# A hybrid encoder on one core: output-weight splits placed behind the last pair's first scores, and one weight sum made by an adding transfer

## The chip, the core and the metric

The kernel runs on one core of a Trainium2 chip. The metric is the device time of one execution in microseconds (us), the median of several runs. A core has TensorE (PE, matmuls; PEld loads the stationary operand), VectorE (DVE), ScalarE (ACT), GpSimd (POOL) and SyncE (SP), each with its own queue of instructions that it works through in order. Transfers are issued from SP and POOL here and run on the core's DMA engines.

## What is computed

Two layers on x of 512 x 1024 floats; layer 0 has mixer A, layer 1 mixer B, and each mixer is followed by a squared-ReLU MLP:

```python
for i in range(2):
    h = rms_norm(x, norm_mix[i])
    x = x + (dilated_mixer if i == 0 else mla_mixer)(h, ...)
    h = rms_norm(x, norm_ffn[i])
    a = relu(h @ ffn_w1[i])
    x = x + (a * a) @ ffn_w2[i]
```

Mixer A projects h to q, k and v of three head groups (8 heads of 128 in each), attends in dilated windows and merges the groups. Mixer B projects to low-rank latents, makes q, k and v of 8 heads from them, scales q and k by their norms, attends over all 512 positions, and multiplies the heads' outputs with b_w_o (1024 x 1024).

## The kernel before, in words

A float32 product is made of three matmuls of rounded operands: each operand is split into a high part (hi, rounded by a copy on ACT, `whi`) and the rest (lo, a subtraction on DVE, `wlo`), and hi·hi, lo·hi and hi·lo are summed in the same bank of PSUM. Lines 157 and 158 make the splits of most weights (`load_unit`), lines 406 and 407 those of mixer A's v weights (`split_w`), line 185 is the matmul of the general projection, line 421 that of the v products.

**Mixer A's v projection** (`v_phase`). The v of a group's heads 0 to 5 is h (512 x 1024) times a 1024 x 768 weight, and it is done by seven products of half-size blocks instead of eight (Strassen's scheme). The weight blocks are b11, b12, b21, b22, each 128 x 4 x 384 on chip (768 KB), loaded by two SP transfers of 384 KB (line 328). `add_block` (line 334) makes sums of blocks with two additions on DVE. In `piece`, for group 0, `bT` holds b11 + b12 for product 5, then has b22 added for product 6, and last b21 for product 4 (the last two in place); product 7 takes b3 = b12 + b22. Ssp0 to Ssp3 are the split sums on the side of h. `put` (lines 438, 440) evacuates the banks into vo, and POOL transfers vo to memory (line 444). The v of head 6, of all three groups at once, is an ordinary projection, whose `raw` weight tiles come by line 145 and whose results (v6) go out by three POOL transfers (line 501). The tiles of the blocks share a set of six buffers ("wq"): a block is loaded when the last reader of an older block has been issued and is done.

**Mixer B** works by pairs of heads. `score` (lines 1105 to 1121) takes one head and 128 rows: five matmuls (three kn, qn; two kr, qr) into one bank, the row-max on DVE (line 1116), its scaling (1117), the exponential on ACT (1119), which reads the bank, and the normalization on DVE (1120, 1121). `part2` transposes the result on PE and copies it to pTs (1130 on ACT, 1132 on DVE); `pv_b` multiplies it with v (1138) and splits the head's output into oB (1140 on ACT, 1141 on DVE). A loop over all scores runs `part2` three scores behind, and makes the next pair's keys and queries between (`kv_chunk`, with ks on line 1086; `q_chunk`, with qn and qr on 1069 to 1073). For the last pair `bank` gives the scores two banks ("sc"), for the others it takes "acc" banks. Then `project` (line 1191) multiplies oB with b_w_o, in units of 128 x 2 x 512: SP loads raw (line 147), ACT and DVE split it (157, 158), and PE adds up the unit's matmuls (185) in four "acc" banks.

**What sets the order.** The program text is recorded and a scheduler then orders the instructions of each engine; a step that is written later can be put earlier where its data and buffers allow. `tc.issue_after(x)` holds a block of the text back: what it holds may not be put ahead of the instruction x on x's engine. The splits of the first b_w_o units, written last, were put among the instructions of the earlier pairs this way.

Of the kernel before, what the change touches and what calls it, by code (L numbers as in the profile page):

```python
# [12 lines left out]
AF = mybir.ActivationFunctionType  # L13
ALU = mybir.AluOpType
AX = mybir.AxisListType
# [4 lines left out]
NT = S // P  # L20
# [4 lines left out]
HB = 8  # L25
# [62 lines left out]
def encoder_kernel(ctx: ExitStack, tc: tile.TileContext, x, norm_mix, norm_ffn, a_w_qkv, a_q_gain, a_k_gain,  # L88
                   a_w_o, b_w_in, b_q_a_gain, b_w_qb, b_kv_a_gain, b_w_kvb, b_q_gain, b_k_gain, b_w_o,
                   ffn_w1, ffn_w2, consts, out):  # L90
    nc = tc.nc
    V, A, G, PE = nc.vector, nc.scalar, nc.gpsimd, nc.tensor
    uid = [0]
    marks = {}

    def nm(s):
        uid[0] += 1
        return f"{s}_{uid[0]}"
# [24 lines left out]
    def transpose(o, i):  # L123
        PE.transpose(o, i, ident)  # L124
# [182 lines left out]
    def v_phase(vp):  # L307
# [23 lines left out]
        def add_block(t, x, y):  # L331
            for u in range(2):
                us = slice(2 * u, 2 * u + 2)
                V.tensor_tensor(t[:, us], x[:, us], y[:, us], op=ALU.add)
# [5 lines left out]
        b11, b21, bT, b12, b22 = {}, {}, {}, {}, {}  # L340
# [83 lines left out]
        def both(p, w, banks, first):  # L424
            for u, t in ((0, 0), (0, 1), (1, 0), (1, 1)):
                product(p, w, banks, first, u, t)

        def new_banks(chain):
            pl, tg = {"a": (sc_p, "sc"), "b": (tp_p, "tp"), "d": (acc_p, "acc")}[chain]
            return [pl.tile([P, 512], F32, tag=tg, name=nm(tg)) for _ in range(2)]  # L430

        def put(g, i, n, how, banks, last):

            o = vo[:, 2 * i + n]
            for t in range(2):
                acc = banks[t][:, :VH]
                if how == "set":
                    A.activation(o[:, t], acc, AF.Copy)
                else:
                    marks["put"] = V.tensor_tensor(o[:, t], o[:, t], acc,  # L440
                                                   op=ALU.add if how == "add" else ALU.subtract).ins
                if last:

                    nc.gpsimd.dma_start(vall[g].rearrange("(m r) d -> m r d", r=NT)
                                        [:, 2 * i + t, VH * n:VH * n + VH], o[:, t])

        def piece(g, ba):

            bb = new_banks("b")
            both(5, bT[g], bb, True)  # L450
            put(g, 1, 1, "set", bb, False)
            add_block(bT[g], bT[g], b22[g])
            both(3, b22[g], bb, False)
            put(g, 0, 1, "set", bb, False)
            b3 = vp.tile([P, 4, VH], F32, tag="h32", name=nm("b3"))
            add_block(b3, b12[g], b22[g])
            both(6, bT[g], ba, False)
            put(g, 0, 1, "sub", ba, True)
            add_block(bT[g], bT[g], b21[g])
            both(7, b3, ba, False)  # L460
            put(g, 1, 1, "sub", ba, True)
            both(4, bT[g], ba, False)
            put(g, 1, 0, "set", ba, True)
# [47 lines left out]
        for i in range(2):  # L511
            split_s(2, dif[:, 1, i], i)
        piece(0, ba)

        rot = vp.tile([P, D], F32, tag="xn", name="rot", bufs=2)
# [435 lines left out]
    if True:  # L951
        with tc.tile_pool(name="bpool", bufs=1, reuse_waits="tile") as bp, \
# [66 lines left out]
            def bank(d, which):  # L1019

                pool, tag = {"s": (sc_p, "sc"), "p": (tp_p, "tp"), "o": (tp_p, "tp")}[which] \
                    if d["p"] == HB // 2 - 1 else (acc_p, "acc")
                return pool.tile([P, 512], F32, tag=tag, name=nm(tag))
# [82 lines left out]
            def score(d, h, r):  # L1106

                qn, qr, kn, kr = d["qn"][r], d["qr"][r], d["kn"], d["kr"]
                rq = d["rq"][:, r, h:h + 1]
                sc = bank(d, "s")  # L1110
                ops = [(qn[:, h, 0], kn[:, h, 0]), (qn[:, h, 0], kn[:, h, 1]), (qn[:, h, 1], kn[:, h, 0]),
                       (qr[:, h], kr[:, h, 0]), (qr[:, h], kr[:, h, 1])]
                for i, (lt, rt) in enumerate(ops):
                    PE.matmul(sc, lhsT=lt, rhs=rt, start=(i == 0), stop=(i == 4))  # L1114
                mx = st.tile([P, 4], F32, tag="bmx", name=nm("bmx"))
                V.tensor_reduce(mx[:, 0:1], sc, axis=AX.X, op=ALU.max)
                V.tensor_scalar(mx[:, 1:2], mx[:, 0:1], rq, -1.0, op0=ALU.mult, op1=ALU.mult)
                pe = bw.tile([P, S], F32, tag="pe", name=nm("pe"), bufs=3)
                A.activation(pe, sc, AF.Exp, bias=mx[:, 1:2], scale=rq, accum_out=mx[:, 2:3])
                V.reciprocal(mx[:, 3:4], mx[:, 2:3])  # L1120
                V.tensor_scalar(pe, pe, mx[:, 3:4], None, op0=ALU.mult)

                def part2(pT):
                    tp = bank(d, "p")
                    for j in range(NT):
                        transpose(tp[:, j * P:(j + 1) * P], pe[:, j * P:(j + 1) * P])
                    tv = tp.rearrange("p (j t) -> p j t", j=NT)
                    dst = pT[:, :, r * P:(r + 1) * P]
                    if r % 2:
                        A.activation(dst, tv, AF.Copy)  # L1130
                    else:
                        V.tensor_copy(dst, tv)
                return part2
# [27 lines left out]
            for s_ in range(HB * NT + lag):  # L1161
                p, c = divmod(s_, 8)
                if s_ < HB * NT:
                    if c == 0 and p:
                        cur = nxt
                    pend.append((cur, c // 4, c % 4, score(cur, c // 4, c % 4)))
                if s_ >= lag:
                    d, h2, r2, f = pend.pop(0)
                    if r2 == 0:
                        if pTs is None:  # L1170
                            pTs = x16.tile([P, 2, NT, S], F32, tag="x16", name="pTs")
                        pT = pTs[:, h2]
                    f(pT)
                    if r2 == NT - 1:
                        pv_b(d, h2, pT)
                if p + 1 < HB // 2:
                    if c == 2:
                        nxt = new_pair(p + 1)
                    if s_ < NT - 1:
                        tail = tail + [q_chunk(cur, s_ + 1)]  # L1180
                    fresh = [fn(nxt, r) for fn, r in plan.get(c, [])]
                    if c == 7:
                        tail, fresh = tail + fresh, []
                    for f in tail:
                        f()
                    tail = fresh

    bh = ctx.enter_context(tc.tile_pool(name="bh", bufs=1, reuse_waits="tile"))
    hT = bh.tile([P, KD, 2, S], F32R, name="hT_f1")
    with tc.tile_pool(name="po1", bufs=1, reuse_waits="tile") as po:  # L1190
        project(oB, b_w_o[0], resid, norm_ffn[1:2, :].rearrange("o d -> (o d)"), hT, po, "g_ffn1")
    with tc.tile_pool(name="mlp1", bufs=1, reuse_waits="tile") as mp:
        mlp(1, ffn_w1[1], ffn_w2[1], hT, resid, mp, lambda r, c: nc.sync.dma_start(
# [33 lines left out]
```

## Time and profile before

| | us |
|---|---|
| median of 3 runs | 1429.62 |
| lowest, highest | 1429.39, 1430.68 |
| the profiled execution | 1427.53 |
| its span | 1425.8 |
| PE busy | 1394.0 |
| DVE busy | 939.6 |
| ACT busy | 740.5 |
| POOL busy | 217.2 |

The span runs from the first instruction to the last in the profile; the execution's time has 1.73 us more. Times of single instructions are counted from the span's start. Matmuls overlap: of a row of matmuls the distance from start to start tells the cost of one (0.17 us for 384 columns, 0.23 for 512), not its duration. The same holds on DVE and ACT, where an instruction begins some 0.08 us before the one ahead of it has ended. A number in square brackets after an instruction is the time for which its engine was idle before it, with what ended the idle time.

### The profile page before, as it was taken

The page shows a single profiled execution, that of the slowest core. Times are in us where ns is not written, and L with a number is a line of the kernel's source. Part 1 is how long each engine was busy: PE and PEld are TensorE (multiplying, and loading weights), DVE is VectorE, ACT ScalarE, POOL GpSimd, SP SyncE. Part 2 cuts the span into 40 slices and gives each one's busy share as a digit, 9 for nine tenths or more (in the row PEclk, how much of TensorE's full clock was granted, in tenths as well). Part 3 has the DMA queues.
Part 4 walks back from the last instruction along what each step waited for, and adds up shares of the span by engine and source line. Part 5 has one row for each costly group of instructions (what it writes and reads, how often), then busy time and mean ns, then how long its engine had stood idle before and what let it go on. Part 6 is the DMA issues. An engine that isn't in the chain of part 4 may idle for free.

```text
span 1425.8 us, 19234 instructions
## 1 busy us (share of the span) xinstructions
PE 1394.0 (98%) x7044; PEld 1183.8 (83%) x7044; DVE 939.6 (66%) x1497; ACT 740.5 (52%) x1594; POOL 217.2 (15%) x240
## 2 busy tenths in 40 slices
PE   7999999999999999999999999999999999999998
PEld 7999888988888988888888887777768888888886
DVE  6886768676886754465564759788745365575647
ACT  6554656464564623553545446677633553544543
POOL 1110212021112001020010203433201020020201
PEclk9999999999999999999999999999999999999999
DMA  9535222322322335668493844200115658394835
GB/s 323 166 134 168 75 87 87 107 89 75 118 61 77 121 134 195 174 133 222 116 233 99 206 120 91 82 31 30 44 40 163 183 127 231 93 234 128 192 90 118
DMA packets 121086, 185.25 MB, mean 130 GB/s; under 512 B 8416, under 2 KB 58336, under 8 KB 120992
## 3 DMA queue, kind: packets, MB, share of 16 engines
q1 hardware_dynamic: 101808, 144.96, 31.6%
q0 software_dynamic: 19184, 39.07, 15.2%
q8 instruction: 55, 0.90, 0.3%
q14 instruction: 39, 0.32, 0.1%
HBM read 176.13 MB, written 7.86 MB: 129 GB/s over the span
## 4 chain that ended last, share of the span: by engine, by line
PE 89%; DVE 6%; ACT 2%; issue 1%; DMA 1%; POOL 0%; SPq 0%; DVEq 0%; ACTq 0%; POOLq 0%
PE acc L185 51%; PE sc L852 11%; PE tp L852 7%; PE tp L124 4%; PE sc L421 3%; PE acc L1138 1%; PE sc L1032 1%; PE acc L1114 1%; PE tp L421 1%; DVE wlo L796 1%; PE sco L701 1%; PE sc L587 1%; PE acc L421 1%; PE sco L697 1%; DVE wlo L407 1%
## 5 line engine op out<-in xcount | busy, mean ns | idle before, releaser
L185 PE MATMUL acc<-whi,hT 128*128 128x512 f32 (+2 forms) x1216 | 384.2, 390 | 2.2 <-ACT hT L739 1.3
L185 PE MATMUL acc<-hT_f,whi 128*128 128x512 f32 (+1 forms) x1152 | 318.7, 366 | 1.7 <-DVE resid L915 1.2
L158 DVE TENSOR_TENSOR wlo<-raw,whi 128x1024 fp32r<-128x1024 f32 (+3 forms) x146 | 172.4, 1189 | 180.2 <-ACT whi L157 179.9
L185 PEld LDWEIGHTS acc<-whi,hT 128*128 128x128 f32 x1216 | 225.4, 188 | 42.0 <-ACT hT L739 1.9
L185 PEld LDWEIGHTS acc<-hT_f,whi 128*128 128x128 f32 x1152 | 208.1, 189 | 37.4 <-DVE resid L915 1.6
L185 PE MATMUL acc<-wlo,hT 128*128 128x512 f32 (+2 forms) x608 | 235.9, 388 | 0.0
L157 ACT ACTIVATE whi<-raw 128x1024 fp32r<-128x1024 f32 (+3 forms) x146 | 149.7, 1031 | 161.5 <-PE acc L185 64.1
L796 DVE TENSOR_TENSOR wlo<-wqs,whi 128x1024 fp32r<-128x1024 f32 x112 | 137.9, 1232 | 113.4 <-ACT whi L795 113.4
L185 PE MATMUL acc<-hT_f,wlo 128*128 128x512 f32 (+1 forms) x576 | 204.9, 366 | 0.0
L795 ACT ACTIVATE whi<-wqs 128x1024 fp32r<-128x1024 f32 x112 | 118.8, 1061 | 161.3 <-PE acc L185 65.8
L852 PE MATMUL sc<-whi,asp 128*128 128x512 f32 x512 | 164.9, 390 | 0.8 <-DVE resid L826 0.7
L781 POOL DMA_DIRECT2D wqs<-in_ffn_w_dram x64 | 77.6, 1344 | 546.1 <-DVE wlo L796 362.4
L185 PEld LDWEIGHTS acc<-wlo,hT 128*128 128x128 f32 x608 | 114.4, 188 | 18.7 <-issue 0.2
L185 PEld LDWEIGHTS acc<-hT_f,wlo 128*128 128x128 f32 x576 | 108.5, 189 | 17.4
L852 PE MATMUL tp<-whi,asp 128*128 128x512 f32 x352 | 112.2, 390 | 1.8 <-DVE resid L826 1.8
L852 PEld LDWEIGHTS sc<-whi,asp 128*128 128x128 f32 x512 | 96.1, 188 | 21.4 <-issue 1.5
L132 POOL TENSOR_TENSOR qrs<-rs_v,nhalf 128x4 f32<-128x4 f32 x48 | 58.7, 1228 | 288.8 <-DVE rs_v L129 239.7
L852 PE MATMUL sc<-wlo,asp 128*128 128x512 f32 x256 | 99.6, 389 | 0.0
L137 ACT ACTIVATE junk<-acc 128x128 f32<-128x128 f32 x192 | 53.0, 276 | 56.4 <-PE acc L185 51.4
L852 PEld LDWEIGHTS tp<-whi,asp 128*128 128x128 f32 x352 | 66.1, 188 | 16.4 <-DVE resid L826 2.7
L852 PE MATMUL tp<-wlo,asp 128*128 128x512 f32 x176 | 68.2, 389 | 0.0
L295 ACT ACTIVATE qkT<-tp 128x512 f32<-128x512 f32 x48 | 35.8, 765 | 51.2 <-PE tp L124 50.9
(231 smaller groups left out, 2185.3 us busy)
## 6 DMA issues: line engine op xcount, KB each, us to landing
wqs<-in_ffn_w_dram SPq DMA_DIRECT2D x80, 512.0 KB, 5.1
raw<-in_ffn_w_dram SPq DMA_DIRECT2D x64, 512.0 KB, 4.5
wqs<-in_ffn_w_dram POOLq DMA_DIRECT2D x64, 512.0 KB, 7.5
raw<-in_a_w_qkv_dram SPq DMA_DIRECT2D x96, 256.0 KB, 3.1
b<-in_a_w_qkv_dram SPq DMA_DIRECT2D x24, 384.0 KB, 5.7
vall<-vo POOLq DMA_DIRECT2D x24, 192.0 KB, 2.2
raw<-in_a_w_o_dram SPq DMA_DIRECT2D x8, 512.0 KB, 3.8
raw<-in_b_w_o_dram SPq DMA_DIRECT2D x8, 512.0 KB, 3.7
```

Of the source, the lines that this page charges most:

```text
L124: PE.transpose(o, i, ident)
L132: G.tensor_tensor(out, v[:, :n], nhalf[:, :n], op=ALU.pow)
L137: A.activation(junk, x, AF.Square, scale=1.0 / math.sqrt(dim), accum_out=out)
L157: A.activation(hi[:, :nk, :n], raw[:, :nk, :n], AF.Copy)
L158: V.tensor_tensor(lo[:, :nk, :n], raw[:, :nk, :n], hi[:, :nk, :n].bitcast(F32), op=ALU.subtract)
L185: PE.matmul(accs[o][:, oc], lhsT=lt, rhs=rt, start=(kt == 0 and p_i == 0 and hv == 0), stop=(kt == total - 1 and p_i == 2), skip_group_che ...
L295: A.activation(dst, tv, AF.Copy)
L421: PE.matmul(banks[t][:, :VH], lhsT=lt, rhs=rt[:, j], start=(first and k == 0 and i_ == 0), stop=(k == 3 and i_ == 2), skip_group_check=True)
L781: marks["sum"] = nc.gpsimd.dma_start(t, src, accum_op=ALU.add).ins
L795: A.activation(hi, x, AF.Copy)
L796: V.tensor_tensor(lo, x, hi.bitcast(F32), op=ALU.subtract)
L852: PE.matmul(bk[t], lhsT=lt, rhs=rt[:, j], start=(first and k == 0 and i_ == 0), stop=(k == 3 and i_ == 2), skip_group_check=True)
```

## The change

Two edits, in `piece` and around the last `project`:

```diff
             put(g, 0, 1, "sub", ba, True)
-            add_block(bT[g], bT[g], b21[g])
+            if g:
+                add_block(bT[g], bT[g], b21[g])
+            else:
+                for u in range(2):
+                    nc.gpsimd.dma_start(bT[g][:, 2 * u:2 * u + 2], wblk(g, 1, 0, u), accum_op=ALU.add)
             both(7, b3, ba, False)
...
-                V.tensor_reduce(mx[:, 0:1], sc, axis=AX.X, op=ALU.max)
+                marks["max"] = V.tensor_reduce(mx[:, 0:1], sc, axis=AX.X, op=ALU.max).ins
...
-                A.activation(pe, sc, AF.Exp, bias=mx[:, 1:2], scale=rq, accum_out=mx[:, 2:3])
+                marks["exp"] = A.activation(pe, sc, AF.Exp, bias=mx[:, 1:2], scale=rq, accum_out=mx[:, 2:3]).ins
...
                     pend.append((cur, c // 4, c % 4, score(cur, c // 4, c % 4)))
+                    if s_ == HB * NT - 8:
+                        last_pair = marks["max"], marks["exp"]
...
-    with tc.tile_pool(name="po1", bufs=1, reuse_waits="tile") as po:
+    with tc.tile_pool(name="po1", bufs=1, reuse_waits="tile") as po, \
+            tc.issue_after(last_pair[0]), tc.issue_after(last_pair[1]):
         project(oB, b_w_o[0], resid, norm_ffn[1:2, :].rearrange("o d -> (o d)"), hT, po, "g_ffn1")
```

The first edit: in group 0 the last of bT's three sums is made by two transfers that read b21 again from memory and add it into bT, issued on POOL (line 464 of the changed file); each reads and writes a half of bT. b21 is then read last by product 2, its buffer is free earlier, and SP's load of group 1's b11 stands ahead of the last raw of the head-6 projection. The second edit: the row-max (DVE) and the exponential (ACT) of the last pair's first score are remembered, and no instruction of the last `project` on these two engines may stand ahead of them.

DVE in group 0, from the split of bT for product 6 on. `b_70` is b3, `b_4` b21, `bT_671` and `b_110` belong to group 1; sc_154 and sc_155 are the banks of products 6, 7 and 4. Before:

```order
L407 TENSOR_TENSOR wlo_546<-bT_384,whi_545 128x2x384
L387 TENSOR_TENSOR Ssp_116<-dif,Ssp_116 128x4x128
L407 TENSOR_TENSOR wlo_562<-bT_384,whi_561 128x2x384
L334 TENSOR_TENSOR bT_384<-bT_384,b_4_122 128x768 x2
L407 TENSOR_TENSOR wlo_584<-b_70_542,whi_583 128x2x384
L334 TENSOR_TENSOR bT_671<-b_84_662,b_85_665 128x768 x2
L407 TENSOR_TENSOR wlo_600<-b_70_542,whi_599 128x2x384
L440 TENSOR_TENSOR vo<-vo,sc_154 128x384
L407 TENSOR_TENSOR wlo_620<-bT_384,whi_619 128x2x384
L440 TENSOR_TENSOR vo<-vo,sc_155 128x384
L407 TENSOR_TENSOR wlo_636<-bT_384,whi_635 128x2x384
L334 TENSOR_TENSOR b_110_824<-b_85_665,b_86_668 128x768 x2
```

and now:

```order
L407 TENSOR_TENSOR wlo_546<-bT_384,whi_545 128x2x384
L334 TENSOR_TENSOR b_70_542<-b_9_143,b_10_146 128x768 x2
L407 TENSOR_TENSOR wlo_562<-bT_384,whi_561 128x2x384
L387 TENSOR_TENSOR Ssp_116<-dif,Ssp_116 128x4x128
L334 TENSOR_TENSOR bT_671<-b_84_662,b_85_665 128x768 x2
L407 TENSOR_TENSOR wlo_584<-b_70_542,whi_583 128x2x384
L440 TENSOR_TENSOR vo<-vo,sc_154 128x384
L407 TENSOR_TENSOR wlo_600<-b_70_542,whi_599 128x2x384
L407 TENSOR_TENSOR wlo_620<-bT_384,whi_619 128x2x384
L440 TENSOR_TENSOR vo<-vo,sc_155 128x384
L334 TENSOR_TENSOR b_110_824<-b_85_665,b_86_668 128x768 x2
L407 TENSOR_TENSOR wlo_636<-bT_384,whi_635 128x2x384
```

The additions bT<-bT,b_4 are gone; b3's additions stand behind the wlo of bT's first half instead of ahead of it (in the first list they are the step just above); wlo_620 and wlo_636 split bT for product 4, and a vo stands behind each.

ACT at the start of the last pair, where pe is the exponential, qn and qr are copies of the transposed queries, and hT the output of the head before. Before:

```order
L1140 ACTIVATE hT_8026<-acc_9574 128x512
L1047 ACTIVATE qs_9486<-sc_9472 128x256
L1069 ACTIVATE qn_9447<-tp_9442,gn 128x2x128
L1072 ACTIVATE qr_9448<-tp_9442 128x256
L1069 ACTIVATE qn_9500<-tp_9495,gn 128x2x128
L1072 ACTIVATE qr_9501<-tp_9495 128x256
L1119 ACTIVATE pe_9526,bmx_9523<-sc_9517,bmx_9523,rqs_76 128x512
L1069 ACTIVATE qn_9511<-tp_9506,gn 128x2x128
L157 ACTIVATE whi_9853<-raw_9851 128x1024
```

and now:

```order
L1145 ACTIVATE hT_8026<-acc_9574 128x512
L1074 ACTIVATE qn_9500<-tp_9495,gn 128x2x128
L1074 ACTIVATE qn_9511<-tp_9506,gn 128x2x128
L1077 ACTIVATE qr_9501<-tp_9495 128x256
L1077 ACTIVATE qr_9512<-tp_9506 128x256
L1124 ACTIVATE pe_9526,bmx_9523<-sc_9517,bmx_9523,rqs_76 128x512
L157 ACTIVATE whi_9725<-raw_9723 128x1024
L157 ACTIVATE whi_9755<-raw_9753 128x1024
L157 ACTIVATE whi_9785<-raw_9783 128x1024
```

The first exponential stood ahead of the last qn and qr and now stands behind both qr; the first three whi of b_w_o, which stood some 30 instructions and more further up, follow it.

PE at the same place: sc_9517, sc_9536 and sc_9555 are the first three scores, acc_9719 to 9722 the four banks of the last projection. Before, around the first score:

```order
L185 MATMUL acc_9720<-whi_9725,hT_8026 128x512
L185 MATMUL acc_9720<-wlo_9726,hT_8026 128x512
L185 MATMUL acc_9720<-whi_9725,hT_8026 128x512
L1114 MATMUL sc_9517<-kn_9160,qn_9387 128x512 x3
L185 MATMUL acc_9720<-whi_9725,hT_8026 128x512
L185 MATMUL acc_9720<-wlo_9726,hT_8026 128x512
```

and now, around the third:

```order
L1119 MATMUL sc_9536<-kr_9161,qr_9448 128x512 x2
L1119 MATMUL sc_9555<-kn_9160,qn_9500 128x512 x3
L1119 MATMUL sc_9555<-kr_9161,qr_9501 128x512 x2
L124 MATMUL tp_9594<-ck,pe_9526 128x128 x4
L185 MATMUL acc_9719<-whi_9725,hT_8026 128x512
L185 MATMUL acc_9720<-whi_9725,hT_8026 128x512
L185 MATMUL acc_9721<-whi_9725,hT_8026 128x512
```

The L185 matmuls stood among the scores, from right behind p·v (line 1138) on, and now begin behind the third score and the first transposes of an exponential; the first two scores' kn matmuls now stand ahead of the p·v of the pair before.

## Rows read from the trace of the kernel before

**Rows 1.** The page, parts 1, 2 and 4: totals, granted clock by slice, chain.

```profile
PE 1394.0 (98%) x7044; PEld 1183.8 (83%) x7044; DVE 939.6 (66%) x1497; ACT 740.5 (52%) x1594; POOL 217.2 (15%) x240
...
PEclk9999999999999999999999999999999999999999
...
PE 89%; DVE 6%; ACT 2%; issue 1%; DMA 1%; POOL 0%; SPq 0%; DVEq 0%; ACTq 0%; POOLq 0%
```

**Rows 2.** Busy time by stretch: us, PE, PEld, DVE, ACT, POOL, PEclk, DMA share, GB/s.

```profile
40.00:45.00 5.00, 5.00 (x31) 5.00 (x30) 5.00 (x7) 3.97 (x6) 2.06 (x3) 1.00 0.17 49
...
50.00:55.00 5.00, 4.98 (x29) 4.66 (x27) 5.00 (x7) 2.93 (x4) 0.00 (x0) 1.00 0.82 298
55.00:60.00 5.00, 3.62 (x21) 3.65 (x22) 5.00 (x7) 1.07 (x2) 1.10 (x2) 1.00 0.32 87
```

**Rows 3.** PE, timeline, group 0: start, us, engine, line, out<-in, [idle before <-releaser].

```profile
56.38 0.41 PE L421 MATMUL sc<-whi,Ssp 128*128 128x384 f32 x1 [1.40 <-DVE vo L440]
...
61.13 0.34 PE L421 MATMUL sc<-whi,hT 128*128 128x384 f32 x1
```

**Rows 4.** PE, timeline, mixer B: the two holes that ks ends.

```profile
970.69 0.41 PE L1032 MATMUL sc<-whi,cT 128*128 128x384 f32 x1 [1.20 <-DVE ks L1086]
...
1003.67 0.41 PE L1032 MATMUL sc<-whi,cT 128*128 128x384 f32 x1 [1.21 <-DVE ks L1086]
```

**Rows 5.** DVE, timeline, mixer B: the splits ahead of ks.

```profile
968.89 1.31 DVE L158 TENSOR_TENSOR wlo<-raw,whi 128x1024 fp32r<-128x1024 f32 x1
970.13 0.41 DVE L1086 TENSOR_TENSOR ks<-sc,krs 128x256 f32<-128x256 f32 x1
...
1001.87 1.32 DVE L158 TENSOR_TENSOR wlo<-raw,whi 128x1024 fp32r<-128x1024 f32 x1
```

**Rows 6.** Busy time from 1005 to 1055, columns as in rows 2.

```profile
1005.00:1055.00 50.00, 50.00 (x238) 38.38 (x237) 33.20 (x84) 25.12 (x64) 7.05 (x10) 1.00 0.15 52
```

**Rows 7.** PE, timeline, end of mixer B.

```profile
1056.66 3.70 PE L1138 MATMUL tp<-pTs,vb 128*128 128x512 f32 x8 [0.69 <-ACT pTs L1130]
1061.04 0.50 PE L185 MATMUL acc<-whi,hT 128*128 128x512 f32 x1 [0.69 <-ACT hT L1140]
```

**Rows 8.** DVE, timeline, group 0: the removed additions and the first vo.

```profile
50.47 1.82 DVE L334 TENSOR_TENSOR bT<-bT,b 128x768 f32<-128x768 f32 x2
...
55.69 0.54 DVE L440 TENSOR_TENSOR vo<-vo,sc 128x384 f32<-128x384 f32 x1
```

**Rows 9.** Instructions of line 501 (copies of v6): durations in ns, transfers.

```profile
L501 POOL DMA_DIRECT2D vall<-v x3: 733/837/946, 42.9 to 44.2; - x3
...
DMA to landing us min/median/max: 2.8/3.3/3.5
```

**Rows 10.** Instructions of line 781 (the MLP's adding transfers, 512 KB each).

```profile
L781 POOL DMA_DIRECT2D wqs<-in_ffn_w_dram x64: 1194/1204/2222, 560.7 to 1404.1; - x64
...
DMA to landing us min/median/max: 5.9/7.5/14.7
```

**Rows 11.** ACT, timeline: the last raw of the head-6 projection.

```profile
30.48 0.85 ACT L157 ACTIVATE whi<-raw 128x768 fp32r<-128x768 f32 x1 [0.89 <-DMA raw<-in_a_w_qkv_dram]
```

**Rows 12.** PE, timeline: its first matmul.

```profile
33.96 0.87 PE L185 MATMUL acc<-whi,hT 128*128 128x384 f32 x4
```

**Rows 13.** PE, timeline, the last pair's start.

```profile
1015.63 3.60 PE L1138 MATMUL acc<-pTs,vb 128*128 128x512 f32 x8
1018.66 0.79 PE L185 MATMUL acc<-whi,hT 128*128 128x512 f32 x1
...
1030.50 0.84 PE L1114 MATMUL sc<-kn,qn 128*128 128x512 f32 x3
```

**Rows 14.** DVE, timeline: the last pair's first row-max.

```profile
1024.29 0.69 DVE L1116 TENSOR_REDUCE bmx<-sc 128x1 f32<-128x512 f32 x1 [1.70 <-PE sc L1114]
```

**Rows 15.** ACT, timeline, the last pair's start.

```profile
1025.53 0.39 ACT L1072 ACTIVATE qr<-tp 128x256 fp32r<-128x256 f32 x1 [1.23 <-DVE qn L1070]
1025.81 0.77 ACT L1119 ACTIVATE pe<-sc,bmx,rqs 128x512 f32<-128x512 f32 x1
```

## The prediction, made before the changed kernel had run

> **What bounds the kernel now.** I read the page's totals first, then the busy time by stretches, then the two places that the change touches, engine by engine. TensorE (PE) is busy 1394.0 of 1425.8 us, its granted clock is in the top tenth in every slice, the 2.4 GHz level, and 89% of the chain that ended last is PE [rows 1]. Only some 32 us are not PE work, and the change removes no matmul: it can only win idle time of PE at its two places, or add some. The profiled execution took 1427.53 us, 1425.8 of span and 1.73 around it, 2.09 below the median of the three runs. I make the sum as a difference to the profiled execution and put it on the median, 1429.62. A difference under 0.2%, 2.86 us, is about what a measurement of this kernel can't tell from none.
>
> Place one, mixer A's group 0, is bound by VectorE: DVE is busy 5.00 of 5 us in each stretch, while PE falls to 3.62 between 55 and 60 [rows 2]. PE stops there once: product 7 starts at 56.38, after 1.40 us of idle that a vo of DVE ends; product 4 follows at 61.13 [rows 3]. Place two, the end of mixer B, is PE-bound with small holes. Two, of 1.20 and 1.21 us, end on the key scaling ks of DVE [rows 4]; directly ahead of each ks DVE did a wlo of b_w_o, from 968.89 to 970.20 and from 1001.87 to 1003.19 [rows 5]. Behind these PE is full from 1005 to 1055 [rows 6]; then come two holes of 0.69 each [rows 7].
>
> **Part one: the weight sum as an adding transfer.** Removed: the two additions at 50.47, 1.82 us of DVE [rows 8]. DVE's work behind them moves up by that, the vo with it, so PE's hole can close: at most 1.40 gained.
>
> Added: two POOL transfers of 384 KB that add into bT; ACT's and DVE's splits of bT for product 4 wait for them. The first may start when DVE has split bT's first half, about 47.8 in the new order, where the two b3 additions stand behind that step; the second after the other half, about 50.4. POOL is free by then: its three copies of v6 start between 42.9 and 44.2 [rows 9]. No transfer of this size that adds is in the trace. The nearest are the MLP's 64 of 512 KB: 1.2 us of POOL each, landing after 5.9, 7.5 and 14.7 us (least, median, most) [rows 10]. I take 7: a quarter fewer bytes than those, but beside a 768 KB load of b22 for group 1. The first half lands at 54.8.
>
> Queued behind the wait are ACT's whi of bT and DVE's wlo of bT, and behind that wlo the vo (0.54) that frees product 7's second bank [rows 8]. Without the wait DVE would begin that wlo near 54.8: an Ssp to 50.85, the two group 1 additions to 52.6, a wlo, a vo and a wlo. With it whi runs to 55.7, wlo to 56.75, vo to 57.2, while PE has done product 7's first bank from 54.9 to 57.0: a hole of some 0.3. The second half lands at 57.4: whi to 58.2; DVE's wlo, behind the two group 1 b3 additions (1.74 at pace, from 57.2), to 59.85; the vo behind it, which frees product 4's bank, to 60.3. Product 4 starts near 60.45 against 61.13: **0.7 gained**. With a landing of 6 or less the gain is the bound, 1.40; from 8.2 on it is a loss, at 9 about 1.4.
>
> b21's buffer comes free earlier, so group 1's b11, 768 KB, is now issued ahead of the last raw of the head-6 projection. At the 298 GB/s of 50 to 55 [rows 2] that is 2.6 us: ACT's whi of that raw, 30.48 to 31.33 [rows 11], would end at 34.0. Its first matmul is at 33.96 [rows 12] and now stands four or five matmuls, 0.7 to 0.9, later. I cost it at nothing; without that cover it is some 0.7, up to DVE's next vo.
>
> One rule speaks against this part. What the rows show: the three copies of v6 were issued while DVE was never idle (5.00 of 5 [rows 2]) and landed in 2.8 to 3.5 us [rows 9]. The Trainium skill, SBUF — State Buffer, section "SBUF: two separate sides", says that while VectorE runs an operation in a two-port mode GpSimd can't write a transfer's descriptors, and the transfer seems blocked by VectorE. By that rule the sum would become that of the third rival; the trace so far speaks against it.
>
> **Part two: the splits of b_w_o behind the last pair's first scores.** Four pairs whi and wlo leave the stream of the earlier pairs, each 1.31 or so on DVE [rows 5]. The holes of 1.20 and 1.21 close; the other two wlo stood where DVE had slack. Walking the new order, part of the 2.41 comes back as short waits on score banks and on pTs, and **1.5 is left** when PE reaches the last pair. Bounds: 2.41 and 0.
>
> At the last pair PE now lacks its filling. Before, 34 matmuls L185 of 0.23 each stood among the first three scores, from 1018.66 to 1030.50 [rows 13]; now they stand behind score 3. PE enters p·v at 1015.63 [rows 13] and needs 3.43 for it; less 1.5, plus 1.37 for six score matmuls (0.23 each) and 0.44 for four transposes that moved ahead of it, it ends at 1019.4. Eight transposes (0.88) and four score matmuls (0.91) give 1021.2. Score 3 then needs the bank of score 1, which the exponential of score 1 frees. That stands behind a row of steps: ACT's and DVE's hT (0.6 each) to 1020.7, the row-max, 0.6 at pace (0.69 in [rows 14]), qn, the second row-max and the second qn (0.4, 0.6, 0.4) to 1022.7, and then on ACT the second qr, which waits for DVE's qn (1.23 of wait at 1025.53 now), and the exp of 0.77 [rows 15]. I get 1024.0, **2.85 of new idle time**. No work covers it, since the first L185 stands behind score 3. Behind it the splits are in time: the first whi (1.1 by the 0.85 of [rows 11] for three quarters of the columns) runs under score 3 and its transposes (1.6), the first wlo under four whi matmuls that stand ahead. The next raw loads start only when a wlo frees their buffer, from 1026 on, and are needed after 1040, so even 10 us would do. The tail holes of 0.69 [rows 7] stay, since what they wait for, pTs and hT of the last head, still comes last. Net: 1.5 − 2.85 = −1.35; the walk rounds each handover up by some 0.05, so I take **1.1 lost**. Bounds: 2.41 gained if the exponential is in time, 2.85 lost if the closed holes all return.
>
> **Sum.** 1429.62 − 0.7 + 1.1 = **1430.0**, not to be told from no change.
>
> **The rivals.**
> - *The transfers win nothing:* DVE exchanges two additions for a wait as long, at a landing of 8.2 to 9. For it: the median of 7.5 [rows 10] is close. Against it: fewer bytes. Time: 1429.62 + 1.1 + 0 to 1.4 = 1430.7 to 1432.1.
> - *The new hole doesn't open:* if the exponential isn't held back by the two qr, part two keeps 1.5 and with part one's 0.7 to 1.40 gives 1427.4 to 1426.7, and with all of 2.41 1425.8. For it: the two closed holes are plain in the rows. Against it: the bank and ACT's order are fixed in the program.
> - *Slower: the adding transfers are held up.* Place: DVE's first wlo of bT, near 55. If their descriptors are written only when DVE pauses, the first half lands 6 to 7 after DVE itself stops to wait, near 62, and product 4 starts at 65 to 66 instead of 61.13: 4 to 5 lost, with part two 1434.7 to 1435.7. The most of 14.7 [rows 10] does the same. It decides from a landing near 10: from there the loss with part two's passes 2.86. Against it: the three copies under a busy DVE [rows 9].
> - *Slower: nothing of the 1.5 arrives,* the closed holes return elsewhere, and part two loses its 2.85 whole: 1431.8 to 1433.
>
> **How the numbers follow.** The forecast has 0.44, all within 0.2%. The transfers win nothing: 0.18, within. No new hole: 0.23, of which 0.12 lies over 0.2% on the fast side. Transfers held up: 0.09, slower. The holes return: 0.06, of which 0.05 slower. That is 0.12 faster, 0.74 the same, 0.14 slower. The range leaves out the held transfers and the lowest corner of the second rival: 1426.4 to 1433.4. The likeliest case alone: 1428.8 to 1431.2.
>
> **What would show it.** Right: no addition of b21 on DVE near 50; a landing near 7; PE's hole ahead of product 7 gone or moved into it with under 0.6, and product 4 near 60.4; no hole of 1.2 ended by ks near 969 and 1001; one new PE hole of 2 to 3 at the third score of the last pair, ended by ACT's exp, and full PE behind it; the granted clock unchanged. Wrong: a landing over 9 with DVE or PE waiting for it; a hole at raw of head 6 near 33; holes over 0.5 with other releasers between 970 and 1018; no hole, or one over 4, at the third score; new holes from 1055 on.

## The result, and the profile after

The changed kernel takes 1433.1 us (median; 1430.81 to 1434.11), the kernel before 1429.24 in the same comparison: a ratio of 1.0025, 95% interval 1.0015 to 1.0034. The time lies within the range of the prediction, 1426.4 to 1433.4, close to its upper end and 3.1 us above its number; the forecast difference was +0.4 us, the measured one is +3.9. 0.25% is a little more than the 0.2% that was called the least to be told from no change, and the interval ends on both sides of it: slower, by a little. The profiled execution took 1433.78 us, its span 1432.0.

The page of the changed kernel, parts 1, 2 and 4, as [rows 1] of before:

```profile
PE 1397.4 (98%) x7044; PEld 1184.7 (83%) x7044; DVE 935.6 (65%) x1495; ACT 740.4 (52%) x1594; POOL 220.6 (15%) x242
...
PEclk9999999999999999999999999999999999999999
...
PE 87%; DVE 6%; DMA 3%; ACT 2%; issue 1%; SPq 0%; POOL 0%; ACTq 0%; DVEq 0%
```

Two additions less on DVE, two transfers more on POOL, the same matmuls. Nothing at this level tells where 6.2 us of span have come from (1432.0 against 1425.8); the two places do.

**Place one.** PE, timeline, around product 4 (the third row is its first matmul):

```profile
55.64 0.41 PE L421 MATMUL sc<-whi,Ssp 128*128 128x384 f32 x1
...
61.19 0.62 PE L421 MATMUL acc<-whi,hT 128*128 128x384 f32 x2 [1.08 <-ACT whi L406]
61.91 0.44 PE L421 MATMUL sc<-whi,hT 128*128 128x384 f32 x1
```

The hole of 1.40 ahead of product 7 [rows 3] is gone: product 7 starts at 55.64. But one of 1.08 stands behind it. ACT's whi that ends it stands right behind the whi of bT's second half, and that one had waited for an adding transfer. ACT, timeline:

```profile
59.56 0.85 ACT L406 ACTIVATE whi<-bT 128x768 fp32r<-128x768 f32 x1 [3.41 <-DMA bT<-in_a_w_qkv_dram]
```

Instructions of line 464, the adding transfers:

```profile
L464 POOL DMA_DIRECT2D bT<-in_a_w_qkv_dram x2: 1229/1233/1237, 49.5 to 52.1; - x2
...
DMA to landing us min/median/max: 5.1/6.3/7.4
```

The landings of 5.1 and 7.4 are about as taken (7). The issue was late: 49.5 and 52.1 where 47.8 and 50.4 had been forecast. The delay began at the last raw of the head-6 projection. ACT and then DVE, timeline:

```profile
33.96 0.85 ACT L157 ACTIVATE whi<-raw 128x768 fp32r<-128x768 f32 x1 [3.65 <-DMA raw<-in_a_w_qkv_dram]
```

```profile
34.84 0.96 DVE L158 TENSOR_TENSOR wlo<-raw,whi 128x768 fp32r<-128x768 f32 x1 [3.20 <-ACT whi L157]
```

In the trace of before the same wlo, behind the whi of [rows 11]:

```profile
31.36 0.96 DVE L158 TENSOR_TENSOR wlo<-raw,whi 128x768 fp32r<-128x768 f32 x1 [1.04 <-ACT whi L157]
```

DVE, which bounds this stage, stood for 3.20 us instead of 1.04. From the start of that wlo to the issue of the first adding transfer it is 14.68 us here, and 14.68 and 14.66 in two other kernels with the same order of part one (part one alone, 33.58 to 48.26; the hole filled, 33.37 to 48.03): the longer DVE waits there, the later the transfer.

**Place two.** PE, timeline, 957 to 1067: every row with a hole, and two p·v that wait for nothing (958.03 and 1018.82), from which distances are taken below.

```profile
958.03 3.59 PE L1143 MATMUL acc<-pTs,vb 128*128 128x512 f32 x8
...
970.95 3.70 PE L1143 MATMUL acc<-pTs,vb 128*128 128x512 f32 x8 [0.69 <-DVE rs_v L129]
...
980.76 0.41 PE L1037 MATMUL sc<-whi,cT 128*128 128x384 f32 x1 [0.44 <-DVE r L1058]
...
983.63 0.47 PE L1037 MATMUL sc<-whi,cT 128*128 128x512 f32 x1 [0.60 <-DVE rs_v L129]
...
990.92 3.70 PE L1143 MATMUL acc<-pTs,vb 128*128 128x512 f32 x8 [0.45 <-ACT pTs L1135]
...
1005.47 0.41 PE L1037 MATMUL sc<-whi,cT 128*128 128x384 f32 x1 [0.21 <-ACT qs L1052]
...
1018.05 0.93 PE L1119 MATMUL sc<-kn,qn 128*128 128x512 f32 x3 [0.86 <-ACT pTs L1135]
1018.82 3.60 PE L1143 MATMUL acc<-pTs,vb 128*128 128x512 f32 x8
...
1026.98 1.27 PE L1119 MATMUL sc<-kn,qn 128*128 128x512 f32 x3 [2.77 <-ACT pe L1124]
...
1062.56 3.70 PE L1143 MATMUL tp<-pTs,vb 128*128 128x512 f32 x8 [0.69 <-ACT pTs L1135]
...
1066.95 0.50 PE L185 MATMUL acc<-whi,hT 128*128 128x512 f32 x1 [0.69 <-ACT hT L1145]
```

The two holes of 1.2 that ks ended [rows 4] are gone, the hole of 2.77 at the third score is there, ended by the exponential, and the tail has kept its two of 0.69 [rows 7]: all as forecast. The forecast also had 0.9 of short waits (2.41 closed, 1.5 left). What came are six other holes between 965 and 1018.1, 3.25 us together, where before had two beside the ks ones, 0.71 together:

```profile
980.20 0.30 PE L124 MATMUL tp<-ck,qs 128*128 128x128 f32 x1 [0.20 <-DVE kr L1103]
...
981.34 0.41 PE L1032 MATMUL sc<-whi,cT 128*128 128x384 f32 x1 [0.51 <-DVE r L1053]
```

So about as much waiting came anew (2.54) as the two closed holes had held. The chain that ends the 2.77, on ACT:

```profile
1024.80 0.38 ACT L1077 ACTIVATE qr<-tp 128x256 fp32r<-128x256 f32 x1 [0.54 <-DVE qn L1075]
1025.79 0.39 ACT L1077 ACTIVATE qr<-tp 128x256 fp32r<-128x256 f32 x1 [0.61 <-DVE qn L1075]
1026.07 0.77 ACT L1124 ACTIVATE pe<-sc,bmx,rqs 128x512 f32<-128x512 f32 x1
```

One thing more in this profile: behind the hole the granted clock falls. Busy time by stretch, columns as in [rows 2]:

```profile
1025.00:1030.00 5.00, 3.02 (x10) 2.47 (x11) 4.51 (x10) 4.39 (x8) 0.00 (x0) 0.74 0.00 0
1030.00:1035.00 5.00, 5.00 (x21) 4.09 (x21) 4.73 (x7) 2.35 (x5) 0.00 (x0) 0.91 0.72 209
```

and PE, timeline, the rows behind the third score's kn: two matmuls take 0.86 from start to start, 0.43 each where 0.23 is the full level's.

```profile
1028.05 1.05 PE L1119 MATMUL sc<-kr,qr 128*128 128x512 f32 x2
1028.91 1.05 PE L124 MATMUL tp<-ck,pe 128*128 128x128 f32 x4
```

**A measure without holes.** Since the profiles start some tenths apart and a hole's number leaves out the end of the matmul ahead of it (the hole of 2.77 costs 2.96 by the measure below), I compare distances between starts of the same matmuls: A is the p·v at 957.23 in the trace of before (958.03 above), B the p·v at 1015.63 [rows 13] (1018.82), C the L185 at 1061.04 [rows 7] (1066.95). PE, timeline of before, A and the p·v behind the first hole of [rows 4]:

```profile
957.23 3.60 PE L1138 MATMUL acc<-pTs,vb 128*128 128x512 f32 x8
...
971.83 3.60 PE L1138 MATMUL acc<-pTs,vb 128*128 128x512 f32 x8
```

In the change, in part two alone and with the hole filled six score matmuls and four transposes, 1.81 us, stand ahead of B instead of behind it. In the three kernels whose hold ends earlier the scores stand otherwise around B, so only A to C is given for them. The kernels are described in the next section.

| kernel | A to B | B to C | A to C |
|---|---|---|---|
| before | 58.40 | 45.41 | 103.81 |
| the change | 60.79 | 48.13 | 108.92 |
| part one alone | 58.39 | 45.43 | 103.82 |
| part two alone | 60.80 | 46.56 | 107.36 |
| hole filled | 60.82 | 46.55 | 107.37 |
| held back, one score earlier | – | – | 107.94 |
| held back, four scores earlier | – | – | 107.99 |
| held back behind the first ks | – | – | 108.43 |
| part one, the raw load first | 58.38 | 45.42 | 103.80 |
| each split behind its ks | 56.96 | 45.40 | 102.36 |
| the same, with part one, the raw load first | 57.00 | 45.40 | 102.40 |

Of the 6.2 us of span 5.11 lie between A and C. Another 0.8 lie in place one, measured in "Part one with the raw load first" below.

### The profile page after: what moved, and what is told of

The parts are those of the page before. It is cut to its first block, busy times and chain, and to the rows that moved or that the text cites. A ratio compares the mean times of both kernels' runs of the same rounds, so it can differ in the third digit from the quotient of the medians.

```text
span 1432.0 us, 19242 instructions
## 1 busy us (share of the span) xinstructions
PE 1397.4 (98%) x7044; PEld 1184.7 (83%) x7044; DVE 935.6 (65%) x1495; ACT 740.4 (52%) x1594; POOL 220.6 (15%) x242
## 4 chain that ended last, share of the span: by engine, by line
PE 87%; DVE 6%; DMA 3%; ACT 2%; issue 1%; SPq 0%; POOL 0%; ACTq 0%; DVEq 0%
PE acc L185 51%; PE sc L857 11%; PE tp L857 7%; PE tp L124 4%; PE sc L421 2%; PE acc L1143 1%; PE acc L1119 1%; PE sc L1037 1%; PE tp L421 1%; DVE wlo L801 1%; DMA raw<-in_a_w_qkv_dram 1%; PE sco L706 1%; PE sc L592 1%; PE sco L702 1%; PE sc L1119 1%
## 5 line engine op out<-in xcount | busy, mean ns | idle before, releaser
L185 PE MATMUL acc<-whi,hT 128*128 128x512 f32 (+2 forms) x1216 | 384.1, 390 | 2.3 <-ACT hT L744 1.4
L185 PE MATMUL acc<-hT_f,whi 128*128 128x512 f32 (+1 forms) x1152 | 319.0, 366 | 1.7 <-DVE resid L920 1.2
L185 PEld LDWEIGHTS acc<-whi,hT 128*128 128x128 f32 x1216 | 225.8, 189 | 42.2 <-ACT hT L744 1.9
L185 PEld LDWEIGHTS acc<-hT_f,whi 128*128 128x128 f32 x1152 | 208.4, 189 | 37.2 <-DVE resid L920 1.6
L185 PE MATMUL acc<-wlo,hT 128*128 128x512 f32 (+2 forms) x608 | 235.9, 388 | 0.2 <-DVE wlo L158 0.2
L185 PE MATMUL acc<-hT_f,wlo 128*128 128x512 f32 (+1 forms) x576 | 205.2, 366 | 0.1
L185 PEld LDWEIGHTS acc<-wlo,hT 128*128 128x128 f32 x608 | 114.4, 188 | 19.0 <-DVE wlo L158 0.5
L185 PEld LDWEIGHTS acc<-hT_f,wlo 128*128 128x128 f32 x576 | 108.6, 189 | 17.8 <-DVE wlo L158 0.3
```

Of the source, the lines that this page charges most:

```text
L185: PE.matmul(accs[o][:, oc], lhsT=lt, rhs=rt, start=(kt == 0 and p_i == 0 and hv == 0), stop=(kt == total - 1 and p_i == 2), skip_group_che ...
```

## The experiments

Two theories of the loss stood against each other at first. H: the hole at the third score and the lower clock behind it make the loss, and the waits ahead of the last pair are in sum what they were. A: part one makes it, by its transfers and by the load that moved ahead of the raw. Later ones (P and D, then 1 and 2) ask whether splits that are held back lose in any case, and whether the gain of the two closed holes can be had. The texts on record give what each theory expects of a run.

**The two parts apart.** Part one alone leaves the hold-back out:

```diff
-    with tc.tile_pool(name="po1", bufs=1, reuse_waits="tile") as po, \
-            tc.issue_after(last_pair[0]), tc.issue_after(last_pair[1]):
+    with tc.tile_pool(name="po1", bufs=1, reuse_waits="tile") as po:
```

> The adding transfer alone; the last projection is not held back. Theory H (the hole ahead of the last pair's third score and the lower clock behind it make the loss): the program is 0.9 us later from group 0 on, as in the changed kernel's trace, and at most 1 us in all: ratio 1.0000 to 1.0010; first matmul of product 4 near 61.9, group 1 0.9 later than before, no idle time of PE over 1 us after 900 that the kernel before does not have, granted clock 1.00 throughout. Theory A (the transfers and the load that moved ahead of the raw make the loss): ratio 1.0020 to 1.0030, most of the changed kernel's 1.0025.

Measured: 1429.05 against 1428.82, ratio 1.0002 (0.9993 to 1.0011). That is in H's range and not in A's. In its trace product 4 starts at 60.68, not near 61.9 as H had it, because the raw came earlier there than in the change (more on this below). Part two alone has the additions on DVE again:

```diff
-            if g:
-                add_block(bT[g], bT[g], b21[g])
-            else:
-                for u in range(2):
-                    nc.gpsimd.dma_start(...)
+            add_block(bT[g], bT[g], b21[g])
```

> The last projection held back behind the last pair's first row-max and exponential; the weight sum on DVE as before. Theory H: the hole of 2.7 to 2.8 us at the third score, ended by the exponential, and a granted clock under 0.8 in the 3 to 4 us behind it, about 1.7 us of matmul time lost; the waits between 965 and the hole sum to about as much as before (3.1), so the end is 4 to 5 later in the profile; ratio 1.0015 to 1.0030. Theory A: ratio 0.9995 to 1.0005, with the closed holes paying for the new one.

Measured: 1432.37, ratio 1.0026 (1.0016 to 1.0037). The loss is part two's: in the table it is 3.55 us from A to C, 0.25% of the time. Its hole at the third score is that of the change, to the hundredth. But the low clock that H expected behind it isn't there; the granted clock is full in this profile (PE, timeline, and busy time by stretch, columns as in [rows 2]):

```profile
1026.96 0.96 PE L1114 MATMUL sc<-kn,qn 128*128 128x512 f32 x3 [2.77 <-ACT pe L1119]
...
1025.00:1030.00 5.00, 3.04 (x15) 2.56 (x16) 4.65 (x11) 4.40 (x8) 0.00 (x0) 1.00 0.00 0
```

**The hole filled with work.** Twelve matmuls whose sums nothing reads are put between the second and the third score, and all else is left (`second` is the last matmul of the second score; the lines that mark it are left out here):

```diff
+            with tc.issue_after(second):
+                fill = acc_p.tile([P, 512], F32, tag="acc", name=nm("fill"))
+                for i in range(12):
+                    PE.matmul(fill, lhsT=cur["qr"][1][:, 0], rhs=cur["kr"][:, 0, 0],
+                              start=(i == 0), stop=(i == 11))
```

> The changed kernel with 12 matmuls of 512 columns that nobody reads, held behind the second score of the last pair, so that they stand in the hole; nothing else moves. Theory H, the hole lowers the clock: the third score starts at about 1027 as in the changed kernel, the granted clock stays 1.00 behind it, and the end comes 1.6 to 1.8 earlier than in the changed kernel: ratio to the kernel before 1.0010 to 1.0018. Rival S, the clock falls for another reason (the matmuls after the hole, or a state of the run): clock under 0.8 behind the third score again, ratio 1.0020 to 1.0035.

Measured: 1433.11, ratio 1.0031 (1.002 to 1.0041). The clock is H's, the time is that of its rival S. PE, timeline:

```profile
1022.65 2.91 PE L1200 MATMUL fill<-kr,qr 128*128 128x512 f32 x12
1025.58 0.97 PE L1119 MATMUL sc<-kn,qn 128*128 128x512 f32 x3
```

No idle time is left there and the clock stays full, and A to C is the 107.37 of part two alone. The p·v at B and the third score are 8.16 us apart as in the change (1017.42 to 1025.58). So the wait costs its length, whether PE idles or works, and the part of H that blames the clock is refuted: the lower clock is not what part two costs. In the change's own profile it came on top: 108.92 less 107.36, 1.56 us. The medians show nothing of such an amount: the change with its hole and the change with the hole filled are at 1.0025 and 1.0031, within each other's intervals.

**Held back less.** Three kernels, without part one, move the point behind which the splits may stand: one score earlier (the last score of the pair before), four scores earlier, and behind the first ks of the last pair's keys. The edit of the first:

```diff
-                    if s_ == HB * NT - 8:
+                    if s_ == HB * NT - 9:
```

> The kernel before with the last projection held back behind the row-max and exponential of the score just ahead of the last pair's first. 14 matmuls of the projection then stand behind the previous pair's p.v and 27 ahead of the third score. Theory H: no idle time of over 1 us at the third score and the clock at 1.00; the waits between 965 and 1018 stay near 3.2 in sum, as in the changed kernel, since they come from the order and not from the hole: ratio 0.9985 to 1.0005. If holding back the splits is bad by itself (late splits, late loads of b_w_o): ratio over 1.0015.

> The kernel before with the last projection held back behind row-max and exponential of the score four ahead of the last pair's first. Nine matmuls of the projection behind p.v, 25 more around score 2. Theory P: third score without a hole of over 1 us, ratio 0.9990 to 1.0010. Theory D: 1.0015 or more.

> The kernel before with the last projection held back only behind the last pair's first key scaling ks (DVE) and the copy of its values (ACT), so that no wlo stands ahead of that ks, and the first score of the last pair comes with its filling: p.v of the pair before and ten matmuls of the projection stand between score 1 and score 3. Theory P (the loss of part two is PE without work at the third score, 2.8 us; the waits of the middle come from the order of the queues): no idle time over 1 us at the third score, total within 1 us of the kernel before, ratio 0.9990 to 1.0008. Theory D (holding splits back is bad by itself: they come too late, with their loads): ratio 1.0015 or more, with waits on whi, wlo or raw in the last pair. If the closed ks holes stay closed: ratio under 0.9990.

Measured: 1431.63, ratio 1.002 (1.0011 to 1.0029); 1435.04, ratio 1.0043 (1.0031 to 1.0056); 1434.79, ratio 1.004 (1.0026 to 1.0053). Theories H and P allowed at most 1.0005 to 1.0010; all three are slower than that, as theory D had it. The hole at the third score is gone in all three, and each has a new one. Their largest, in this order:

```profile
1018.01 0.70 PE L1114 MATMUL sc<-kn,qn 128*128 128x512 f32 x2 [1.76 <-DVE r L1053]
```

```profile
1008.55 3.70 PE L1138 MATMUL acc<-pTs,vb 128*128 128x512 f32 x8 [3.32 <-ACT pTs L1130]
```

```profile
1003.20 0.63 PE L124 MATMUL acc<-ck,pe 128*128 128x128 f32 x4 [2.51 <-DVE pe L1121]
```

Wherever the hold ends, three whi of ACT and three wlo of DVE stand within 6 to 8 us, among and ahead of steps that PE waits for. And all three have the small holes of 0.69, 0.44 or 0.45, 0.61 and 0.45 at about 970, 980, 983 and 990 that the change has. So these don't depend on where the hold ends. That they come from the order which the scheduler makes once the first split isn't there is an inference.

**Part one with the raw load first.** Group 1's b11 is held behind the last raw load on SP, everything else in the text as in part one alone (`last_raw` is the last issue of that load; the lines that mark it are left out here):

```diff
-            b11[g] = block(g, 0, 0, "b11")
+            with tc.issue_after(last_raw):
+                b11[g] = block(g, 0, 0, "b11")
```

> The adding transfer alone, with the load of group 1's b11 held behind the last raw of the head-6 projection, as its place was before. If the late raw (whi of it 33.96 against 30.48) is what delays DVE's splits and so the issue of the transfers: the transfers are issued 1 us or more earlier than the 49.5 and 52.1 of the changed kernel, the hole ahead of product 4 shrinks from 1.08 to under 0.5, and the program is 0.5 to 1.4 earlier than the kernel before from group 1 on; ratio 0.9985 to 1.0003. If the transfers' landing alone decides (5.1 and 7.4 us), the hole stays near 1 and the ratio is 1.0000 to 1.0010, like part one alone.

Measured: 1428.38 against 1429.19, ratio 0.9996 (0.9987 to 1.0005), the first kernel of this study below 1, though not to be told from it. The order of DVE changed with it: b3's additions stand ahead of the first of bT's two wlo again, and the transfers are issued at 48.8 and 50.3. The raw's whi on ACT; then, on PE, a hole in product 7 ahead of its second bank, and the first matmul of product 4:

```profile
30.18 0.85 ACT L157 ACTIVATE whi<-raw 128x768 fp32r<-128x768 f32 x1 [0.48 <-DMA raw<-in_a_w_qkv_dram]
```

```profile
57.25 0.45 PE L422 MATMUL sc<-whi,Ssp 128*128 128x384 f32 x1 [0.63 <-DVE vo L441]
...
59.97 0.41 PE L422 MATMUL sc<-whi,hT 128*128 128x384 f32 x1 [0.34 <-DVE vo L441]
```

Again a distance, from the first L421 to the hole in group 1 that a vo ends. PE, timeline of before:

```profile
11.06 0.69 PE L421 MATMUL acc<-whi,hT 128*128 128x384 f32 x1 [0.69 <-ACT hT L373]
...
86.54 0.41 PE L421 MATMUL sc<-whi,Ssp 128*128 128x384 f32 x1 [0.62 <-DVE vo L440]
```

That is 75.48. With the transfers it is 76.26 in the change (whi of the raw at 33.96), 74.99 in part one alone (32.70), 74.66 in the kernel with the filled hole (32.49), and with the raw first 74.65 (30.18). Against before's one profile the transfers win 0.5 to 0.8 where the raw comes by 32.7, and lose 0.8 where it comes at 34. But the kernels without the transfers spread as well: 74.94 to 75.72 in the six profiles of this study, 75.3 in the mean. So the change's 76.26 lies above all of them, in one profile, while the gain, about 0.5 in the mean, is no larger than their spread.

**The splits kept, each behind its ks.** The theory by now: the two 1.2-us holes are worth having, but are to be had by an exchange of two neighbours on DVE, not by taking the splits away. The four splits stay among the earlier pairs, and the first two are held behind the third ks on DVE, and the third copy of the values (vb) on ACT, of the third pair, the next two behind those of the last pair. Part one is left out.

```diff
-        A.activation(hi[:, :nk, :n], raw[:, :nk, :n], AF.Copy)
-        V.tensor_tensor(lo[:, :nk, :n], raw[:, :nk, :n], hi[:, :nk, :n].bitcast(F32), op=ALU.subtract)
+        held = marks.get("wo")
+        ks_, vb_ = held.pop(0) if held else (None, None)
+        with (tc.issue_after(ks_) if ks_ else contextlib.nullcontext()), (tc.issue_after(vb_) if vb_ else contextlib.nullcontext()):
+            A.activation(hi[:, :nk, :n], raw[:, :nk, :n], AF.Copy)
+            V.tensor_tensor(lo[:, :nk, :n], raw[:, :nk, :n], hi[:, :nk, :n].bitcast(F32), op=ALU.subtract)
...
+    marks["wo"] = [marks["own%d" % (HB // 2 - 2)]] * 2 + [marks["own%d" % (HB // 2 - 1)]] * 2
```

> Part one as before; the four splits of b_w_o stay among the earlier pairs, but the first (whi, wlo) may not stand ahead of the third ks of its pair, nor the third ahead of the third ks of the last pair: on DVE the order ks, wlo takes the place of wlo, ks, and the last pair's scores keep their L185 filling. Theory 1 (the two 1.2-us holes are a cost of the splits, and what loses in the change is the third score alone): both holes close, the last pair is as before, 1.5 to 2.4 faster, ratio 0.9983 to 0.999. Theory 2 (the waits of this stretch only move: what is taken from ks comes back at the next handover, an rs_v, pTs or r): the 1.2-us holes close, holes of 0.4 to 0.9 with other releasers appear between 970 and 1018, sum of waits 965 to 1018 within 0.5 of the 3.1 of before, ratio 0.9995 to 1.0005.

Measured: 1427.28 against 1428.73, ratio 0.9993 (0.9984 to 1.0002). DVE, timeline, then PE's holes from 960 to 1020:

```profile
970.38 0.41 DVE L1090 TENSOR_TENSOR ks<-sc,krs 128x256 f32<-128x256 f32 x1
970.71 1.21 DVE L162 TENSOR_TENSOR wlo<-raw,whi 128x1024 fp32r<-128x1024 f32 x1
```

```profile
972.49 3.70 PE L1144 MATMUL acc<-pTs,vb 128*128 128x512 f32 x8 [0.27 <-ACT pTs L1136]
...
982.11 0.41 PE L1036 MATMUL sc<-whi,cT 128*128 128x384 f32 x1 [0.51 <-DVE r L1057]
...
1004.74 3.70 PE L1144 MATMUL acc<-pTs,vb 128*128 128x512 f32 x8 [0.26 <-ACT pTs L1136]
```

1.04 us of holes where before had 3.12 (0.20 and 0.51, at 980.20 and 981.34, beside [rows 4]), and A to B is 1.44 shorter. The sum of the holes speaks against theory 2, which had it within 0.5 of 3.1, and for theory 1 in the main: both holes close, though two of 0.27 and 0.26 come anew. The ratio lies between the two theories' ranges, and the median, 1.45 lower, could not alone tell the gain from no change. Theory 1's aside that the third score alone loses in the change doesn't hold: part two loses 0.6 ahead of B too. With part one and the raw load first:

> As split_behind_its_ks, with part one's adding transfers and group 1's b11 held behind the last raw load (part1_raw_first, 0.9996). Theory 1: 2 to 3 faster than before, ratio 0.998 to 0.9987. Theory 2: as part1_raw_first, 0.999 to 1.0000. Neither expects a difference between the two kernels of this call of more than 0.001.

Measured: 1427.13 against 1428.73, ratio 0.9988 (0.9979 to 0.9997), 1.6 us less: the one kernel whose whole interval is below 1, if barely. The ratio is just above theory 1's range and just below theory 2's.

## Why the prediction was right and wrong

That the time fell into the range is in part luck. The range was wide enough to hold the fourth rival, to which 0.06 was given; the likeliest case, 1428.8 to 1431.2, is missed by 1.9 us, and the time isn't "not to be told from no change" but slower by 0.25%. The forecast of part two was 1.1 lost and 3.55 came; that of part one was 0.7 won, and no median shows it.

**The hole at the third score: right.** Forecast 2.85 from the chain hT, row-max, qn, row-max, qn, qr, exp; the trace has 2.77 with the same chain, and 8.16 us from the start of p·v to the third score where the forecast had 8.0 (1019.4 less 3.43 to 1024.0). From B to C part two alone takes 46.56 where before without the moved 1.81 takes 43.60: 2.96 lost. No work behind it gave anything back, as said.

**"1.5 is left" of the closed holes: wrong, and this step made most of the difference.** The two holes closed, but from A to B part two alone takes 60.80, and before with the moved 1.81 would take 60.21: 0.6 lost where 1.5 was to be won, a term wrong by 2.1. With 2.96 that is the 3.55 of the table, where the forecast had 1.1 to 1.35. It is what the fourth rival said, with a chance of 0.06: nothing of the 1.5 arrives, the closed holes return elsewhere. The prediction's own sign for this is there too, holes over 0.5 with other releasers between 970 and 1018: 0.69, 0.60 and 0.86. What the trace shows of how: before, six projection matmuls stood between the hole at 970.69 [rows 4] and the next p·v, which began at 971.83 without a wait. In the new order that p·v, at 970.95, stands ahead of the six and waits itself. Its row names rs_v of DVE, but what it reads is pTs, and ACT's copy of that ended last, at 970.90:

```profile
970.30 0.60 ACT L1135 ACTIVATE pTs<-acc 128x512 f32<-128x512 f32 x1 [0.31 <-PE acc L124]
```

There the handover from ACT to PE has no filling any more; the other five places were not followed in this way. In the walk I checked the two holes that I knew and rounded the rest; the new order had to be read as a new program. That the gain was there is shown by the splits kept behind their ks: 1.44, close to the 1.5 forecast, but in an order of PE that is nearly that of before. That the order, and not the missing splits themselves, made the new holes is argued from the three earlier holds and not separated further.

**Part one's 0.7: the mechanism right, one cost left out.** The transfers landed in 5.1 to 7.4 against 7 and the hole ahead of product 7 closed. Where the raw was in time, product 4 came at 59.97 (forecast 60.45), with a hole of 0.63 within product 7 (forecast some 0.3). The step that failed is "I cost it at nothing": the whi of the raw ended between 33.3 and 34.8 in three profiles, around the 34.0 worked out, but I looked for the cover on PE alone (four or five matmuls). The stage is bound by DVE, and DVE's wlo of that raw waited 2.16 us longer (3.20 against 1.04); the first transfer was issued at 49.5 where it was 48.0 in the kernel with the filled hole, whose whi began at 32.49. The runs of part one alone, 1.0002 (0.9993 to 1.0011), show no gain, but their interval would still hold 0.7 us, a ratio of 0.9995: whether part one wins anything stays open.

**The rivals.** "The transfers win nothing" fits the median of part one alone (1.0002) and isn't shown by it; a landing of 8.2 to 9, its condition, did not come. "The new hole doesn't open" is refuted by the 2.77. "The adding transfers are held up" fell: DVE was busy 5.00 of 5 us from 50 to 55 in the changed kernel too, and the two transfers landed in 5.1 and 7.4 us. The rule of the Trainium skill, SBUF — State Buffer, section "SBUF: two separate sides", by which they would have been held up, speaks of DVE's two-port operations. DVE ran nothing but TENSOR_TENSOR in those 5 us, and the prediction had no row to show that these are such operations; no run here tests the rule.

## What to carry to other kernels

Price a hold-back by what stands behind it as well as ahead of it: splits taken out of slack come back close together in front of something that waits, as they did at all four points where a hold ended here. Where a wait names one instruction behind another on the same engine, exchange these two and leave the rest of the order alone; that won 1.44 us in the traces, in a stretch where moving all four splits lost 0.6. And where a load is made later, look for its cover on the engine that bounds the stage, not on the one that uses the result.

## What the runs showed of the hardware

The granted clock behind a hole isn't settled by the hole: behind 2.77 us of idle PE it read 0.74 in 1025 to 1030 in the changed kernel and 1.00 in part two alone with the same hole. In the first, matmuls behind it took 0.43 each against 0.23, the lower of the two levels, 1.2 GHz, for some 3 us. Nor is it settled by the hole's length: it read 1.00 in every stretch of 5 us from 1000 to 1035 in the kernels with holes of 3.32 and 2.51, and it fell behind holes of 1.76 and 0.73 in the kernel held back one score earlier, whose next eight matmuls took 4.83 us from start to start (1019.78 to 1024.61) where before they took 3.03 (1015.63 to 1018.66):

```profile
1020.00:1025.00 5.00, 5.00 (x9) 1.99 (x8) 3.58 (x9) 1.91 (x5) 2.31 (x2) 0.66 0.71 228
```

What decides between the two was not tried.

The same load, in the same place of the program, came at quite different times: the last raw let ACT's whi begin at 33.96, 32.70 and 32.49 in three profiles of part one's order. From 32.49 to 33.96, 1.47 us, the way to group 1's hole grew by 1.60. Without the transfers, and with the raw's whi between 30.32 and 31.61, that way still differs by up to 0.78 from profile to profile.
